# Value reload splits moved back, table loads given a later due time, and one query tile moved ahead of mixer A, in a one-core encoder layer

## The chip, the core and the metric

The kernel runs on one core of one Trainium2 chip. The metric is the device time of one execution in microseconds (us), a median over several executions. The engines are named as in the profile: PE (TensorE matmul) and PEld (its weight loads), DVE (VectorE), ACT (ScalarE), POOL (GpSimd) and SP (SyncE, which here only issues DMAs). Each engine takes its instructions in the order of the program and waits at semaphores for the others.

## The reference

One encoder layer over 512 tokens of width 1024: two token mixers side by side, merged by gates, then a SwiGLU channel mixer, with layer norm after each half.

```python
proj = h @ w_in[l]
qa, ka, va, qb, kb, vb = jnp.split(proj, SPLITS, axis=-1)
# partial rotary on qa, ka, qb, kb
o_a = windowed_gqa_sink(qa, ka, va, a_sink[l])      # 16 query heads, 4 key heads, |i-j| <= 128
o_b = dilated_mixture(qb, kb, vb)                   # 3 groups of 4 heads, strides 1, 4, 16
gates = jax.nn.sigmoid(h @ w_gate[l] + b_gate[l])
g_a, g_b = jnp.split(gates, N_BRANCH, axis=-1)
mixed = g_a * (o_a @ w_br_a[l]) + g_b * (o_b @ w_br_b[l])
h = layer_norm(DN_ALPHA * h + mixed @ w_out[l], ln1_g[l], ln1_b[l])
f = (jax.nn.silu(h @ w_ff_gate[l]) * (h @ w_ff_up[l])) @ w_ff_down[l]
h = layer_norm(DN_ALPHA * h + f, ln2_g[l], ln2_b[l])
```

## The kernel before

Everything is float32. To keep its precision on PE, each operand is split into a high part (a copy rounded to `fp32r`, L332 on ACT or L334 on DVE) and a low part (source minus high part, a subtraction on DVE), and a product is three matmuls: high by high, high by low, low by high. A dense projection of 128 output features is 8 such triples, 24 matmuls of 128x512 (`feat_k`, L453 to L455).

The kernel is written as a list of operations that a small planner (`Program.run`) puts in order when the program is built. The planner has a cost for each operation and a priority: for most, the planned PE time at which the operation was written down plus an offset (`prio`, where `EV` is -100, so "100 us early"), for some an absolute number (`abs_prio`). At each moment of its own clock it gives each engine the ready operation with the lowest number for which slots and banks are free. What comes out is one fixed order for each engine. On the chip an engine can't overtake: if the planner thought that a transfer would land earlier than it does, everything behind its reader on that engine waits.

`ORDER` is the list of steps of the first half. `q2` to `q7` and `k1` are projections for mixer A, `VA` the values of mixer A together with those of mixer B's first group, `G` and `g` a gate projection, `T` a "turn" (rotary on up to four tiles at once), and `A0` to `A3` the four key heads of mixer A with 4 query blocks each. The projections k0, q0 and q1 stand ahead of the list. The `Q`, `K`, `V` and `B` words are mixer B.

Four places matter here.

- **Tables and mask.** `ropec`, `ropes` (for the turn), `maska`, `sink`, `ident` and `bgate` are loaded through SP at L340, after the input and the first weights and close to the weights of q2 and of `VA` (L609).
- **Values and their reload.** `token_values(False)` makes four 128x512 tiles of values. Each is copied out of PSUM and stored to DRAM (`va`, L638). When all four are stored, they are read back in another order of rows: four loads of 128x256 for mixer A (L644), then eight of 64x256, two to a tile, for the first group of mixer B (L650). Each of the four tiles is then split twice by `value_split` (high part L332 or L334, low part L588): the first splits take the L644 halves and are needed by `A0`, the second splits take the L650 halves and are needed by mixer B only, some 200 us later.
- **A unit of mixer A** (`unit_a`): for each of 4 heads a pair of score matmuls (L575, L576) into a bank, a masked reduction on DVE (L724), an exponential on ACT (L728); then a reciprocal on DVE (L731) and four normalisations (L664 on ACT or L666 on DVE); then transposes on PE (L676), whose result is copied and split (L332 on ACT, L681 on DVE), and the products with the values (L741, L742).
- **The turn.** The raw rows go through SP (L482) into one tile, DVE shuffles and combines them with the tables (L493 to L499), SP moves them back (L503), and the heads are split (L525, L541).

Of the kernel before, what the change touches and what calls it, by code (L numbers as in the profile page):

```python
# [15 lines left out]
P = 128  # L16
S = 512
# [28 lines left out]
PE, ACT, DVE, POOL, SP = "PE", "ACT", "DVE", "POOL", "SP"  # L46
# [25 lines left out]


ORDER = """
q2 VA T G A0 q3 q4 G k1 T A1 q5 G q6 q7 T A2 G G A3 Q00 K00 T V Q02 K02 T Q01 K01 T B0 B1 G g Q10 K10 T g Q12 K12 T Q11 K11 T B2 B3 g8
"""


# [18 lines left out]
class Program:  # L97
# [72 lines left out]
    def run(self):  # L170
# [5 lines left out]
        dma = [0.0, 0.0]  # L176
# [22 lines left out]
        while n_left:  # L199
# [11 lines left out]
            while progress:  # L211
                progress = False
                for e in engines:
# [25 lines left out]
                    if e == SP:  # L239
                        end = now + 0.06  # L240
                        dma[0] = max(dma[0], now) + (0.45 if cost > 0.2 else 0.62)
                        dma[1] = max(dma[1], dma[0] + 0.65) + cost
                        o.done = dma[1] + 0.9
                    elif o.moves:
                        end = now + cost
                        dma[1] = max(dma[1], end) + o.moves
                        o.done = dma[1] + 2.0
                    else:
                        end = now + cost
                        o.done = end  # L250
# [28 lines left out]
def dve(n, fast=False, extra=0.0):  # L279
    return 0.069 + (0.00074 if fast else 0.00104) * n + extra  # L280
# [7 lines left out]
def hybrid_layer(ctx: ExitStack, tc: tile.TileContext, wpack, xT, xtok, sink, bgate,  # L288
# [140 lines left out]
        op([(DVE, dve(S))], lambda e, j=j, st=st: nc.vector.tensor_tensor(  # L429
            xl[j](), st.t, f32(xh[j]()), op=ALU.subtract), reads=[st, th], writes=[tl], abs_prio=ap)  # L430
    cosT, sinT, mA, mB = slot(), slot(), slot(), slot()
    for t_, src, ap in ((cosT, ropec, -119.3), (sinT, ropes, -119.2)):
        load(t_, src[0:16].unsqueeze(0).broadcast_to([8, 16, S]), abs_prio=ap)
    load(mA, maska, abs_prio=-119.3, dst=lambda: mA.t[:, :384])
    load(nsink, sink.partition_broadcast(P), 0.1, abs_prio=-119.2)
    load(ident, identd, 0.2, abs_prio=-119.1)
    load(bg, bgate, 0.1, abs_prio=-119)
    op([(DVE, 0.08)], lambda e: nc.vector.tensor_scalar(nsink.t, nsink.t, -1.0, None, op0=ALU.mult),
       reads=[nsink], writes=[nsink], abs_prio=-119)
# [23 lines left out]
        for k in range(KD):  # L463
            feat_k(ps, wu, k, XM, xtok_of)

    EV, NOW = -100.0, -300.0


    SHUF = [*range(8, 16), *range(0, 8), *range(24, 32), *range(16, 24)]
# [1 line left out]
    class Turn:  # L471
# [16 lines left out]
        def turn(self):  # L488
            n = len(self.m)
            t, w = self.t, slot()  # L490
            r = slice(0, 32 * n)
            toks = [(t, i, hh) for i in range(n) for hh in range(2)]
            op([(DVE, dve(S, extra=0.03))], lambda e: nc.vector.stream_shuffle(w.t[r], t.t[r], SHUF), reads=toks,  # L493
               writes=[w], prio=EV)
            op([(DVE, dve(S))], lambda e: nc.vector.tensor_tensor(t.t[r], t.t[r], cosT.t[r], op=ALU.mult),
               reads=[*toks, cosT], writes=[t], prio=EV)
            op([(DVE, dve(S))], lambda e: nc.vector.tensor_tensor(w.t[r], w.t[r], sinT.t[r], op=ALU.mult),
               reads=[w, sinT], writes=[w], prio=EV)
            op([(DVE, dve(S))], lambda e: nc.vector.tensor_tensor(t.t[r], t.t[r], w.t[r], op=ALU.add),  # L499
               reads=[t, w], writes=[t], prio=EV)  # L500
            for i, (raw, heads, post, args) in enumerate(self.m):
                for hh in range(2):
                    op([(SP, 0.1)], lambda e, raw=raw, a=64 * hh, d=32 * i + 16 * hh: nc.sync.dma_start(  # L503
                        raw.t[a:a + 16], t.t[d:d + 16]), reads=[t, raw], writes=[(raw, hh)], prio=EV)
                post(raw, heads, *args)
# [72 lines left out]
        return go, [(qt, "h"), (qt, "l"), (kt, "h"), (kt, "d"), (kl, "h"), (kl, "d")]  # L578


    def value_split(ps, c0, toks):

        t = slot(F32R)
        v = lambda: t.t.rearrange("p (h c) -> p h c", h=4)
        src = lambda: ps.t[:, c0:c0 + 256].rearrange("p (h c) -> p h c", h=4)
        op(cp_alts(256, True), lambda e: copy(e, v()[:, :, 0:64], src()), reads=toks,
           writes=[(t, "h"), (t, "room")], prio=EV)
        op([(DVE, dve(256))], lambda e: nc.vector.tensor_tensor(  # L588
            v()[:, :, 64:128], src(), f32(v()[:, :, 0:64]), op=ALU.subtract),
           reads=[*toks, (t, "h")], writes=[(t, "l")], prio=EV)  # L590
        return t

    def vtok(t):
# [2 lines left out]
    def token_values(dilated):  # L596
# [43 lines left out]
        if not dilated:  # L640
            raw = [slot() for _ in range(NR)]
            every = [(aside, r) for r in range(NR)]
            for m, t in enumerate(raw):
                op([(SP, 0.37)], lambda e, t=t, m=m: nc.sync.dma_start(  # L644
                    t.t[:, 0:256], aside.t[:, 32 * m:32 * m + 32, 0:256]), reads=every, writes=[(t, 0)], prio=EV)

            for m, t in enumerate(raw):
                for h in range(2):
                    c = 16 * ((2 * m - 1 + h) % 8)
                    op([(SP, 0.18)], lambda e, t=t, h=h, c=c: nc.sync.dma_start(  # L650
                        t.t[64 * h:64 * h + 64, 256:512], aside.t[:, c:c + 16, 256:512]), reads=every, writes=[(t, 1, h)],
                       prio=EV)
            for g in range(2):
                for m, t in enumerate(raw):
                    res[g].append(value_split(t, 256 * g, [(t, 1, h) for h in range(2)] if g else [(t, 0)]))
        return res


# [937 lines left out]
```

## Time and profile before

| | |
|---|---|
| median of 3 runs | 792.73 us (792.34 to 793.79) |
| profiled execution | 792.01 us, of which the span is 790.2 us |
| PE busy | 770.3 us (97%) |
| DVE, ACT busy | 651.1 us (82%), 482.6 us (61%) |
| weight loads on PE busy | 677.4 us (86%) |
| DMA queue of SP | 91.47 MB, 35.7% of 16 engines |

The span runs from the first instruction to the last; the 1.8 us that the profiled execution has over it lie around it. Times inside the span are counted from its start. In rows of the timeline the columns are start, length, engine and line, operation, out<-in with shapes, and in brackets the idle time of the engine just before, with what ended it. A matmul's length overlaps the next one: what it costs is the distance between two starts, 0.23 us for 128x512 at the full clock. A row of the windows view has the stretch, its length, and for each engine the busy time with the number of instructions, then the granted PE clock, the DMA share and GB/s. A row of the waits view has the waiting engine and line, what it waited for, and total, number and longest wait. Line numbers are those of the kernel before; in the changed kernel the same lines stand one to three further down.

### The profile page before, as it was taken

How to read it: one execution, taken by the hardware profiler on the slowest of the kernel's cores; microseconds unless marked ns; L12 is line 12 of the kernel's file. 1: busy time of each engine (PE TensorE's matmuls, PEld its weight loads, DVE VectorE, ACT ScalarE, POOL GpSimd, SP SyncE). 2: the span in 40 equal slices, each digit the busy share in tenths (PEclk: the TensorE clock that was granted, in tenths of full speed). 3: DMA queues.
4: the chain of work that ended last, by engine and by line, in shares of the span. 5: the costliest groups of instructions: out<-in, count | busy, mean ns of one | idle time of the engine just before them, and what ended most of it. 6: DMA issues, size and time to landing. Idle time of an engine off the chain costs nothing.

```text
span 790.2 us, 13367 instructions
## 1 busy us (share of the span) xinstructions
PE 770.3 (97%) x4470; PEld 677.4 (86%) x4470; DVE 651.1 (82%) x1370; ACT 482.6 (61%) x1066; POOL 124.1 (16%) x288
## 2 busy tenths in 40 slices
PE   8996999999999999999999999999999999999996
PEld 5785888888888888888888899999999999999985
DVE  5385887988899999688686999888888889788697
ACT  5455667778687787596252557655655655555631
POOL 0010000001001701600011011134112330123002
PEclk9997999999999999999999999999999999999999
DMA  7744222313132225154465188779876987689202
GB/s 243 216 151 152 84 79 93 100 46 117 38 106 92 82 82 169 55 188 158 139 206 109 50 216 251 174 171 202 221 197 149 227 203 210 168 221 201 66 1 107
DMA packets 69221, 113.36 MB, mean 143 GB/s; under 512 B 8608, under 2 KB 17440, under 8 KB 69152
## 3 DMA queue, kind: packets, MB, share of 16 engines
q1 hardware_dynamic: 57488, 91.47, 35.7%
q0 software_dynamic: 11520, 20.98, 16.3%
q8 instruction: 35, 0.57, 0.3%
q14 instruction: 34, 0.28, 0.1%
q10 hardware_dynamic: 144, 0.07, 0.0%
HBM read 104.87 MB, written 4.72 MB: 139 GB/s over the span
## 4 chain that ended last, share of the span: by engine, by line
PE 89%; DMA 5%; SPq 3%; ACT 2%; DVE 1%; issue 1%; DVEq 0%; ACTq 0%
PE ps L453 10%; PE ps L454 10%; PE ps L455 9%; PE ps L1310 9%; PE ps L1309 9%; PE ps L1308 9%; PE ps L1437 4%; PE ps L1438 4%; PE ps L1439 4%; PE ps L676 3%; PE ps L1075 3%; PE ps L1074 3%; PE ps L1073 3%; PE ps L576 1%; PE ps L575 1%; PE ps L742 1%
## 5 line engine op out<-in xcount | busy, mean ns | idle before, releaser
L332 ACT ACTIVATE sl<-sl 128x512 fp32r<-128x512 f32 (+4 forms) x452 | 243.5, 568 | 82.9 <-PE ps L454 21.3
L1192 DVE TENSOR_TENSOR sl<-sl,sl 128x512 fp32r<-128x512 f32 (+3 forms) x304 | 170.0, 604 | 10.8 <-ACT sl L332 7.5
L332 ACT ACTIVATE sl<-ps 128x256 f32<-128x256 f32 (+4 forms) x202 | 88.1, 455 | 102.0 <-PE ps L1310 66.0
L453 PE MATMUL ps<-x,sl 128*128 128x512 f32 x304 | 121.9, 401 | 1.0 <-ACT x L332 1.0
L454 PE MATMUL ps<-x,sl 128*128 128x512 f32 x304 | 119.8, 394 | 0.3 <-DVE x L429 0.2
L455 PE MATMUL ps<-x,sl 128*128 128x512 f32 x304 | 119.2, 392 | 0.0
L353 DVE TENSOR_TENSOR sl<-sl,sl 128x512 fp32r<-128x512 f32 x114 | 75.4, 686 | 8.7 <-ACT sl L332 7.9
L1262 POOL DMA_DIRECT2D sl<-wpack x44 | 40.7, 982 | 266.3 <-DVE sl L1192 109.4
L1308 PE MATMUL ps<-x,sl 128*128 128x256 f32 x264 | 74.8, 283 | 0.0
L1310 PE MATMUL ps<-x,sl 128*128 128x256 f32 x264 | 74.7, 283 | 0.0
L1309 PE MATMUL ps<-x,sl 128*128 128x256 f32 x264 | 74.7, 283 | 0.0
L1192 DVE TENSOR_TENSOR sl<-sl,ps 128x512 f32<-128x512 f32 (+1 forms) x78 | 47.4, 611 | 25.7 <-PE ps L1310 16.6
L455 PEld LDWEIGHTS ps<-x,sl 128*128 128x128 f32 x304 | 57.4, 189 | 12.7
L453 PEld LDWEIGHTS ps<-x,sl 128*128 128x128 f32 x304 | 57.7, 190 | 11.3 <-ACT x L332 1.5
L454 PEld LDWEIGHTS ps<-x,sl 128*128 128x128 f32 x304 | 57.6, 190 | 10.4 <-DVE x L429 1.2
L1309 PEld LDWEIGHTS ps<-x,sl 128*128 128x128 f32 x264 | 50.6, 192 | 0.5
L1308 PEld LDWEIGHTS ps<-x,sl 128*128 128x128 f32 x264 | 50.6, 192 | 0.5
L1310 PEld LDWEIGHTS ps<-x,sl 128*128 128x128 f32 x264 | 50.6, 192 | 0.0
L1310 PE MATMUL ps<-tw,sl 128*128 128x256 f32 x176 | 49.8, 283 | 0.0
L1309 PE MATMUL ps<-tw,sl 128*128 128x256 f32 x176 | 49.8, 283 | 0.0
L1310 PE MATMUL ps<-sl,sl 128*128 128x256 f32 x176 | 49.8, 283 | 0.0
L1308 PE MATMUL ps<-tw,sl 128*128 128x256 f32 x176 | 49.8, 283 | 0.0
(150 smaller groups left out, 1862.7 us busy)
## 6 DMA issues: line engine op xcount, KB each, us to landing
sl<-wpack SPq DMA_DIRECT2D x235, 256.0 KB
sl<-wpack POOLq DMA_DIRECT2D x44, 256.0 KB, 5.3
wf<-wpack SPq DMA_DIRECT2D x36, 256.0 KB
wf<-wpack POOLq DMA_DIRECT2D x36, 256.0 KB, 6.4
sl<-sl SPq DMA_DIRECT2D x88, 32.0 KB
sl<-wpack SPq DMA_DIRECT2D x19, 128.0 KB
sl<-xT SPq DMA_DIRECT2D x8, 256.0 KB
sl<-xtok SPq DMA_DIRECT2D x8, 256.0 KB
```

What stands on the lines that cost most here:

```text
L332: nc.scalar.activation(dst, src, AF.Copy)
L353: op([(DVE, dve(S))], lambda e: nc.vector.tensor_tensor(l.t, src.t, f32(h.t), op=ALU.subtract), reads=[src, h], writes=[l], prio=prio, abs ...
L453: mm(o, a, x0, start=(k == 0), stop=False)
L454: mm(o, a, x1, start=False, stop=False)
L455: mm(o, b, x0, start=False, stop=(k == nk - 1))
L1192: op([(DVE, dve(w))], lambda e: nc.vector.tensor_tensor(dst(), x(), y(), op=o), reads=reads, writes=writes, prio=prio)
L1262: return op([(POOL, 1.0)], lambda e: nc.gpsimd.dma_start(dst.t, wpack[u, :, j * S:(j + 1) * S], accum_op=ALU.add), reads=[dst], writes=[ds ...
L1308: mm(o, wh, bh[k](), start=(first and k == 0), stop=False, skip_group_check=True)
L1309: mm(o, wh, bl[k](), start=False, stop=False, skip_group_check=True)
L1310: mm(o, wl, bh[k](), start=False, stop=(k == 3), skip_group_check=True)
L1437: mm(ps.t, x0, w[0].t, start=(first and m == 0), stop=False, skip_group_check=True)
L1438: mm(ps.t, x0, w[1].t, start=False, stop=False, skip_group_check=True)
```

## The change

`ORDER` gets q3 ahead of `A0` instead of behind it. The second value splits get the priority `LATER` (30 us behind the place where they are written) in place of `EV`, and so, in the planner, do the loads that feed them. The planner is told that the reload takes longer: a higher cost for each transfer and 4 us more before its data are there (`READ`). The tables and the mask get `abs_prio` -95.3 to -95.1 in place of -119.3 to -119.1; the load of `bgate` keeps -119. The shuffle of the turn now names the whole tile among what it reads.

```diff
 ORDER = """
-q2 VA T G A0 q3 q4 G k1 T A1 q5 G q6 q7 T A2 G G A3 Q00 K00 T V Q02 K02 T Q01 K01 T B0 B1 G g Q10 K10 T g Q12 K12 T Q11 K11 T B2 B3 g8
+q2 VA T G q3 A0 q4 G k1 T A1 q5 G q6 q7 T A2 G G A3
+Q00 K00 T V Q02 K02 T Q01 K01 T B0 B1 G g Q10 K10 T g Q12 K12 T Q11 K11 T B2 B3 g8
 """
...
-                        o.done = dma[1] + 0.9
+                        o.done = dma[1] + 0.9 + o.moves
...
-    for t_, src, ap in ((cosT, ropec, -119.3), (sinT, ropes, -119.2)):
+    for t_, src, ap in ((cosT, ropec, -95.3), (sinT, ropes, -95.2)):
...
-    load(mA, maska, abs_prio=-119.3, dst=lambda: mA.t[:, :384])
-    load(nsink, sink.partition_broadcast(P), 0.1, abs_prio=-119.2)
-    load(ident, identd, 0.2, abs_prio=-119.1)
+    load(mA, maska, abs_prio=-95.3, dst=lambda: mA.t[:, :384])
+    load(nsink, sink.partition_broadcast(P), 0.1, abs_prio=-95.2)
+    load(ident, identd, 0.2, abs_prio=-95.1)
...
-    EV, NOW = -100.0, -300.0
+    EV, NOW, LATER, READ = -100.0, -300.0, 30.0, 4.0
...
-            op([(DVE, dve(S, extra=0.03))], lambda e: nc.vector.stream_shuffle(w.t[r], t.t[r], SHUF), reads=toks,
+            op([(DVE, dve(S, extra=0.03))], lambda e: nc.vector.stream_shuffle(w.t[r], t.t[r], SHUF), reads=[*toks, t],
...
-                op([(SP, 0.37)], lambda e, t=t, m=m: nc.sync.dma_start(
-                    t.t[:, 0:256], aside.t[:, 32 * m:32 * m + 32, 0:256]), reads=every, writes=[(t, 0)], prio=EV)
+                op([(SP, 0.6)], lambda e, t=t, m=m: nc.sync.dma_start(
+                    t.t[:, 0:256], aside.t[:, 32 * m:32 * m + 32, 0:256]), reads=every, writes=[(t, 0)], prio=EV, moves=READ)
...
-                    op([(SP, 0.18)], lambda e, t=t, h=h, c=c: nc.sync.dma_start(
+                    op([(SP, 0.75)], lambda e, t=t, h=h, c=c: nc.sync.dma_start(
                         t.t[64 * h:64 * h + 64, 256:512], aside.t[:, c:c + 16, 256:512]), reads=every, writes=[(t, 1, h)],
-                       prio=EV)
+                       prio=LATER, moves=READ)
...
-                    res[g].append(value_split(t, 256 * g, [(t, 1, h) for h in range(2)] if g else [(t, 0)]))
+                    res[g].append(value_split(t, 256 * g, [(t, 1, h) for h in range(2)] if g else [(t, 0)],
+                                              LATER if g else EV))
```

What the planner makes of it is seen in three places.

SP, where the tables are loaded. Before, from the last input tile to the first value weights:

```order
L340 DMA sl_108<-xT 128x512
L340 DMA sl_110<-ropec 128x1x512
L340 DMA sl_112<-maska 128x384
L340 DMA sl_114<-ropes 128x1x512
L340 DMA nsink<-sink 128x16
L340 DMA ident<-identd 128x128
L340 DMA bg<-bgate 128x16
L340 DMA sl_121<-maskb 128x512
L340 DMA sl_180<-wpack 128x512
L340 DMA sl_186<-wpack 128x512
L609 DMA sl_188<-wpack 128x2x128 x2
```

The same place of the change:

```order
L341 DMA sl_108<-xT 128x512
L341 DMA bg<-bgate 128x16
L341 DMA sl_111<-ropec 128x1x512
L341 DMA sl_113<-maska 128x384
L341 DMA sl_115<-ropes 128x1x512
L341 DMA nsink<-sink 128x16
L341 DMA ident<-identd 128x128
L341 DMA sl_121<-maskb 128x512
L341 DMA sl_180<-wpack 128x512
L341 DMA sl_186<-wpack 128x512
L610 DMA sl_188<-wpack 128x2x128 x2
```

The tables and the mask stay ahead of the value weights; only the 8 KB load of `bgate` changed its place. Behind this point SP's order is the same up to and with the eight loads of the reload (L650).

PE, where mixer A begins: the end of the first gate (`ps_568`) and what follows. Before:

```order
L455 MATMUL ps_568<-x_199,sl_521 128x512
L575 MATMUL ps_630<-sl_454,sl_470 128x256
L576 MATMUL ps_630<-sl_455,sl_470 128x256
L575 MATMUL ps_638<-sl_454,sl_476 128x256
L576 MATMUL ps_638<-sl_455,sl_476 128x256
L453 MATMUL ps_643<-x_128,sl_528 128x512
```

In the change (`ps_630` is now q3's bank, and the rows are the first six of its 24 matmuls):

```order
L456 MATMUL ps_568<-x_199,sl_521 128x512
L454 MATMUL ps_630<-x_128,sl_528 128x512
L455 MATMUL ps_630<-x_136,sl_528 128x512
L456 MATMUL ps_630<-x_128,sl_529 128x512
L454 MATMUL ps_630<-x_128,sl_528 128x512
L455 MATMUL ps_630<-x_136,sl_528 128x512
L456 MATMUL ps_630<-x_128,sl_529 128x512
```

All of q3 now stands ahead of the first scores. Between those first scores and the first transposes of mixer A there were 30 dense matmuls (q3 and the first 6 of q4) and 16 score matmuls; now there are the same 16 score matmuls and 27 dense ones (all of q4 and the first 3 of a gate).

ACT, up to the first normalisations (L664, in the change L666). The four tiles of the reload are `sl_616`, `sl_618`, `sl_620` and `sl_622`. Before:

```order
L332 ACTIVATE sl_700<-sl_622 128x4x64
L332 ACTIVATE sl_708<-sl_572 128x512
L332 ACTIVATE sl_717<-sl_616 128x4x64
L728 ACTIVATE sl_655,st_653<-sl_655,st_653 128x257
L728 ACTIVATE sl_693,st_715<-sl_693,st_715 128x385
L332 ACTIVATE sl_734<-sl_618 128x4x64
L664 ACTIVATE sl_641<-sl_641,st_653 128x256
L332 ACTIVATE sl_743<-sl_620 128x4x64
L664 ACTIVATE sl_647<-sl_647,st_653 128x256
L664 ACTIVATE sl_649<-sl_649,st_653 128x256
L664 ACTIVATE sl_655<-sl_655,st_653 128x256
L332 ACTIVATE sl_760<-sl_622 128x4x64
```

In the change:

```order
L333 ACTIVATE sl_707<-sl_618 128x4x64
L333 ACTIVATE sl_715<-sl_620 128x4x64
L730 ACTIVATE sl_688,st_692<-sl_688,st_692 128x257
L333 ACTIVATE sl_727<-sl_622 128x4x64
L730 ACTIVATE sl_690,st_692<-sl_690,st_692 128x257
L333 ACTIVATE sl_735<-sl_591 128x512
L730 ACTIVATE sl_694,st_692<-sl_694,st_692 128x257
L333 ACTIVATE sl_764<-sl_618 128x4x64
L666 ACTIVATE sl_682<-sl_682,st_692 128x256
L666 ACTIVATE sl_688<-sl_688,st_692 128x256
L666 ACTIVATE sl_690<-sl_690,st_692 128x256
L333 ACTIVATE sl_781<-sl_599 128x512
```

The second splits of the first two tiles stood ahead of the normalisations (`sl_717`, `sl_734`), and that of the third (`sl_743`) between the first normalisation and the other three. Now one second split on ACT, that of the second tile (`sl_764`), stands ahead of three normalisations in a row; the fourth normalisation went to DVE, behind the subtraction that ends the same split, and the second splits of the third and fourth tile come after it.

More of the change, by code (lines that the diff above doesn't have):

```diff
@@ L578, in scores, with value_split @@
         return go, [(qt, "h"), (qt, "l"), (kt, "h"), (kt, "d"), (kl, "h"), (kl, "d")]
-    def value_split(ps, c0, toks):
+    def value_split(ps, c0, toks, prio=-100.0):
         t = slot(F32R)
@@ L586, in value_split @@
         op(cp_alts(256, True), lambda e: copy(e, v()[:, :, 0:64], src()), reads=toks,
-           writes=[(t, "h"), (t, "room")], prio=EV)
+           writes=[(t, "h"), (t, "room")], prio=prio)
         op([(DVE, dve(256))], lambda e: nc.vector.tensor_tensor(
             v()[:, :, 64:128], src(), f32(v()[:, :, 0:64]), op=ALU.subtract),
-           reads=[*toks, (t, "h")], writes=[(t, "l")], prio=EV)
+           reads=[*toks, (t, "h")], writes=[(t, "l")], prio=prio)
         return t
```

## The prediction

> **What bounds the kernel now.** I read the page first, then PE's waits, then the windows, and last the timelines of PE, ACT and DVE around the one large gap.
>
> ```profile
> span 790.2 us, 13367 instructions
> PE 770.3 (97%) x4470; PEld 677.4 (86%) x4470; DVE 651.1 (82%) x1370; ACT 482.6 (61%) x1066; POOL 124.1 (16%) x288
> ```
>
> PE is busy in all but 20 us of the span. The work on PE is the same before and after, so the change can only win time in which PE stands still or runs slowly. Who makes PE wait is in the waits of PE (total, times, longest):
>
> ```profile
> PE ps L676 <- ACT sl L664: 7.8, 3, 5.8
> PE ps L626 <- ACT sl L332: 1.5, 1, 1.5
> ```
>
> The transposes of mixer A (L676) wait for the normalisations on ACT (L664). The second row is the value projection, which waits once for a weight split. The windows put a place and a clock to both:
>
> ```profile
> 30.00:37.00 7.00, 5.30 (x22) 3.85 (x21) 2.10 (x4) 2.04 (x5) 0.00 (x0) 1.00 0.59 179
> 67.60:69.80 2.20, 0.16 (x1) 0.00 (x0) 1.11 (x4) 0.93 (x4) 0.00 (x0) 1.00 0.27 93
> 69.90:80.00 10.10, 5.00 (x15) 3.70 (x16) 7.54 (x21) 8.32 (x23) 1.15 (x5) 0.50 0.50 158
> 80.30:335.00 254.70, 254.70 (x1307) 216.48 (x1306) 221.04 (x559) 188.39 (x452) 44.01 (x184) 1.00 0.28 88
> 345.00:790.20 445.20, 437.37 (x2833) 399.86 (x2831) 376.55 (x693) 243.37 (x509) 75.18 (x84) 1.00 0.65 166
> ```
>
> From 80.3 to 335 us PE never waits (254.70 busy of 254.70). Behind 345 us it idles 7.8 us in 445, most of it at the very end, and from about 350 us on the order of PE, ACT and DVE is the same in both kernels. The gap is at 67.6 to 80, and the clock is at 0.50 in most of it. PE's timeline there:
>
> ```profile
> 58.10 0.39 PE L455 MATMUL ps<-x,sl 128*128 128x512 f32 x1
> 58.33 0.28 PE L575 MATMUL ps<-sl,sl 128*128 128x256 f32 x1
> ...
> 67.37 0.39 PE L455 MATMUL ps<-x,sl 128*128 128x512 f32 x1
> 73.57 0.48 PE L676 MATMUL ps<-ident,sl 128*128 128x128 f32 x1 [5.81 <-ACT sl L664]
> 75.48 2.13 PE L676 MATMUL ps<-ident,sl 128*128 128x128 f32 x7 [1.43 <-ACT sl L664]
> 77.26 0.78 PE L453 MATMUL ps<-x,sl 128*128 128x512 f32 x1
> 77.83 0.63 PE L454 MATMUL ps<-x,sl 128*128 128x512 f32 x1
> ...
> 80.26 0.40 PE L454 MATMUL ps<-x,sl 128*128 128x512 f32 x1
> 80.49 0.39 PE L455 MATMUL ps<-x,sl 128*128 128x512 f32 x1
> ...
> 83.00 1.03 PE L676 MATMUL ps<-ident,sl 128*128 128x128 f32 x8
> ```
>
> At the full clock a dense matmul takes 0.23 us (80.26 to 80.49). Eight transposes take 0.87 (83.00 to 83.79 where the next matmul starts behind the last two, 0.11 each). Between 67.60 (67.37 and 0.23) and 80.26 PE did 8 transposes and 7 dense matmuls: 0.87 + 7 x 0.227 = 2.46 us of work in 12.66 us. **The gap costs 10.2 us.** Why ACT is late is in its own timeline:
>
> ```profile
> 65.49 0.42 ACT L332 ACTIVATE sl<-sl 128x256 fp32r<-128x256 f32 x1 [4.33 <-DMA sl<-va]
> 68.35 0.42 ACT L332 ACTIVATE sl<-sl 128x256 fp32r<-128x256 f32 x1 [1.95 <-DMA sl<-va]
> ...
> 69.77 0.94 ACT L332 ACTIVATE sl<-sl 128x256 fp32r<-128x256 f32 x2 [0.51 <-DMA sl<-va]
> 71.28 0.42 ACT L332 ACTIVATE sl<-sl 128x256 fp32r<-128x256 f32 x1 [0.57 <-DMA sl<-va]
> ...
> 72.70 0.42 ACT L332 ACTIVATE sl<-sl 128x256 fp32r<-128x256 f32 x1
> 73.02 0.49 ACT L664 ACTIVATE sl<-sl,st 128x256 f32<-128x256 f32 x1
> 74.61 0.42 ACT L332 ACTIVATE sl<-sl 128x256 fp32r<-128x256 f32 x1 [1.09 <-DMA sl<-va]
> 74.93 1.29 ACT L664 ACTIVATE sl<-sl,st 128x256 f32<-128x256 f32 x3
> 76.30 0.42 ACT L332 ACTIVATE sl<-sl 128x256 fp32r<-128x256 f32 x1
> ```
>
> The 128x256 copies are the value splits. The reloaded tiles arrive one by one, about 1.43 us apart: the first halves at 65.5, 66.9 (taken by DVE, shown below), 68.3 and 69.7, the second at 71.2, 72.7, 74.6 and at the latest 76.3. ACT and DVE take them in program order, so each exponential and normalisation behind a split waits for a landing that mixer A does not need.
>
> **The change part by part.** *Tables and mask behind the value weights.* By the order of SP this does not happen: they stay ahead, and only the 8 KB of `bgate` moves in front of them. So the wait at 33 us, the only one that earlier value weights could shorten, stays. The chain of waits shows what the swap can do:
>
> ```profile
> 13.17 7.48 DMA sl<-ropes
> 20.67 0.37 SPq L609
> ```
>
> A value-weight load is issued when `ropes` has landed; `ropes` now goes out one small load later, but one more value-weight load may go out ahead of that landing. Bounds: 0.4 us either way (0.45 us is one issue on SP); I take 0. The tables' own reader, the shuffle at 40 us, is covered by 20 us. The shuffle's extra read and the planner's costs add no instruction: 0.
>
> *q3 ahead of A0, second splits later.* Instruction counts stay; what counts is when PE reaches the transposes and when they may run. Before, PE needed 9.27 us from 58.33 to 67.60 for 30 dense and 16 score matmuls. By the order it now has 51 dense (24 + 27) and the same 16: 21 x 0.23 = 4.8 us more, so it arrives at 72.4. It isn't stopped on the way: the banks that the scores go to now are waited for at reductions that DVE, stepping through its rows, ends 2 us and more ahead of PE. q3's weights were split by 57 us, since q3 ran at 58.8 before without a wait.
>
> When may the transposes run? ACT still has one second split ahead of them, that of the second tile, whose data land at 72.7, the same time as before, since SP's order up to the reload is the same. Its step is 0.32 (72.70 to 73.02), and three normalisations follow at 0.40 each (1.29 for three): ready at 73.5, 73.9 and 74.3. The fourth is on DVE:
>
> ```profile
> 66.92 0.29 DVE L334 CAST sl<-sl 128x256 fp32r<-128x256 f32 x1 [5.29 <-DMA sl<-va]
> ...
> 73.15 0.43 DVE L588 TENSOR_TENSOR sl<-sl,sl 128x256 fp32r<-128x256 f32 x1 [0.24 <-ACT sl L332]
> 73.49 0.61 DVE L724 CUSTOM_DVE_ANT_0 sl<-ps,sl,nsink 128x384 f32<-128x384 f32 x1
> 80.66 0.74 DVE L666 TENSOR_SCALAR sl<-sl,st 128x384 f32<-128x384 f32 x2
> ```
>
> DVE has two reductions of 0.54 each to do from 72.5 on (ready when the last exponential on ACT is done), then the subtraction (0.34) and the normalisation (0.33 for 384 wide, some 0.25 for 256): 74.3. So the last of the first four transposes starts at about 74.4 instead of 72.7: **1.7 us remain.** Of the same kind, smaller: behind the normalisations ACT has a weight split (0.52) and two exponentials (0.6 each) ahead of the copies of the transposed tile (76.5), DVE ends the low part at 77.6, and PE, which by then has 13 more matmuls done, is there at 77.0; with the second product **0.5 us**. The transposes of the next block wait some **0.3 us** for their last normalisation. Together 2.5 us. Bounds for this remainder: 1.1 us (the first transpose alone, 73.5 against 72.4) and 7 us (all four behind the last landing at 76.3, and the clock lost).
>
> No single remaining wait is as long as the one that lowered the clock. By the rows that one had stood 2.2 us (67.6 to 69.8) when the clock fell to 0.50; the value projection's wait of 1.5 us left it at 1.00. So the half-speed stretch goes too.
>
> The sum against the profiled execution: 792.01 - 10.2 + 2.5 = 784.3. The median of the runs lies 0.72 above that execution, so **785.0**.
>
> [...]
>
> **What is late next, and the rivals.** PE reaches everything behind 80 us 7.7 us earlier, and DVE with 221.04 us of work in 254.70 has 13% of slack there, 10.5% in a stretch that is 7.7 us shorter. The tightest place I find is the turn of q3, q4 and k1 ahead of `A1`:
>
> ```profile
> 103.56 0.69 DVE L334 COPY sl<-ps 128x512 f32<-128x512 f32 x1 [0.15 <-PE ps L455]
> ...
> 113.32 0.69 DVE L525 TENSOR_TENSOR sl<-sl,sl 64x512 fp32r<-64x512 f32 x1
> ```
>
> From the end of k1 (103.5) to q3's first head (114.0) it takes 10.5 us. By the order PE has 33 dense matmuls, 20 transposes, 8 score and 10 value matmuls in between: 7.5 + 2.2 + 0.9 + 2.3 = 12.9 us. It is covered with 2.4 us to spare.
>
> - **Part of the wait comes back behind A0** (a late copy of k1, DVE behind its plan, or a longer wait at the first transposes, since five weight loads instead of three now follow the reload at once). For it: the planner that missed the reload by several us made this order too. Against it: PE did not wait once in the 255 us that were planned in the same manner. Price: a wait of 2 us more and 2 us of half clock: 785.0 + 4 = 789.0 (786 to 790.5).
> - **DVE becomes the bound between 80 and 335 us** and everything is given back. It would need the 33.7 us that DVE idles there to be unavoidable. Result: within 1.5 us of 792.7.
> - **Slower: the turn ahead of A1 holds PE.** PE can't pass the first scores of q3's head. The copy of k1 stands on DVE behind a dozen rows of `A0`; if it slips by x, PE waits x - 2.4 us, and with the half clock 2 us more. It is slower than before from x = 2.4 + 7.7 + 1.6 - 2 = 9.7 us; at x = 11 the time is 792.7 - 7.7 + 8.6 + 2 = 795.6.
> - **All of the gap goes**, because the second tile's landing is earlier than its reader showed: 792.7 - 10.2 = 782.5.
>
> **How the numbers follow.** Forecast 785.0 (783.5 to 786): 0.62. Part comes back: 0.18. DVE takes it all: 0.08. Slower: 0.06. Nothing remains: 0.06. A measurement of this kernel tells about 0.2% (1.6 us) from no change. Faster by more: 0.62 + 0.18 + 0.06 = 0.86; within: 0.08; slower: 0.06. The range 782.5 to 790.0 holds the forecast, the last case and most of the first rival, and both bounds of the remainder (2.5 - 7 = -4.5, so 789.5) and of the swap on SP.
>
> **What would show it.** Right: PE's waits name L676 (now three lines down) with under 2.5 us in place of 7.8; no row with a clock of 0.50 between 5 and 785 us; q3 from 58.3 to 63.8, the first transposes at 73 to 74.5, the next block's at about 81.5; PE busy without a gap from there to 335 us; the wait at 33 us as before. Wrong: half clock near 75 us, or a new wait of PE above 2 us at L575 ahead of `A1`, or DVE over 95% busy with PE waiting for it.

## The result, and the profile after

| | before | changed |
|---|---|---|
| median | 792.56 us (792.34 to 793.79, 4 runs) | 783.40 us (782.55 to 785.39, 4 runs) |
| profiled execution | 792.01 us, span 790.2 | 783.75 us, span 782.0 |
| PE idle in the span | 19.9 us | 13.0 us |

The ratio is 0.9885, 95% interval 0.9863 to 0.9907. In one of the experiments below (the cost alone) the profiled execution was disturbed from beginning to end (1548.76 us); that run's time is the median of its three others, and the times in its profile are not used.

The head of the page of the changed kernel, and who makes its PE wait (total, times, longest):

```profile
span 782.0 us, 13402 instructions
PE 769.0 (98%) x4470; PEld 675.1 (86%) x4470; DVE 646.8 (83%) x1364; ACT 484.3 (62%) x1072; POOL 125.9 (16%) x288
...
PE ps L678 <- ACT sl L666: 1.4, 1, 1.4
PE ps L627 <- ACT sl L333: 1.2, 1, 1.2
...
PE ps L454 <- ACT sl L333: 0.4, 1, 0.4
PE ps L744 <- DVE sl L683: 0.2, 1, 0.2
```

The transposes (L676 before, L678 now) waited 7.8 us in three pieces; one piece of 1.4 us is left. PE's work is the same (4470 matmuls); six instructions went from DVE to ACT. The windows of the changed kernel (stretch, length, then busy time and number for PE, PEld, DVE, ACT, POOL, then the granted clock, DMA share, GB/s):

```profile
30.00:37.00 7.00, 5.53 (x24) 4.03 (x23) 2.04 (x3) 2.35 (x4) 0.00 (x0) 1.00 0.65 187
58.00:72.00 14.00, 14.00 (x68) 11.71 (x66) 7.07 (x20) 6.42 (x17) 0.56 (x3) 1.00 0.44 155
72.00:76.00 4.00, 2.49 (x14) 1.79 (x14) 3.54 (x12) 3.36 (x10) 0.53 (x1) 1.00 0.95 252
76.00:82.00 6.00, 5.76 (x28) 4.26 (x27) 4.96 (x13) 5.97 (x14) 0.74 (x4) 1.00 0.37 120
82.00:327.00 245.00, 245.00 (x1265) 208.57 (x1264) 214.73 (x551) 188.19 (x458) 45.80 (x184) 1.00 0.29 89
```

From 58 to 72 us PE never stops; it idles 1.51 us in 72 to 76 and 0.24 in 76 to 82; the clock stays at 1.00; and from 82 to 327 us it is busy for 245.00 of 245.00. (At the very end the clock falls to 0.50 in both kernels, at 776.5 us here and at 786.7 before; PE has started its last matmul by then, at 773.9 and 782.2 us.) The rows of PE, ACT and DVE at the place itself:

```profile
71.76 0.39 PE L456 MATMUL ps<-x,sl 128*128 128x512 f32 x1
73.51 1.67 PE L678 MATMUL ps<-ident,sl 128*128 128x128 f32 x8 [1.36 <-ACT sl L666]
...
81.43 1.03 PE L678 MATMUL ps<-ident,sl 128*128 128x128 f32 x8
...
72.64 0.42 ACT L333 ACTIVATE sl<-sl 128x256 fp32r<-128x256 f32 x1 [0.97 <-DMA sl<-va]
72.97 1.29 ACT L666 ACTIVATE sl<-sl,st 128x256 f32<-128x256 f32 x3
...
73.64 0.42 DVE L589 TENSOR_TENSOR sl<-sl,sl 128x256 fp32r<-128x256 f32 x1
73.98 0.34 DVE L668 TENSOR_SCALAR sl<-sl,st 128x256 f32<-128x256 f32 x1
```

ACT stands 0.97 us for one landing (the second half of the second value tile), splits it, and only then normalises. That is the one second split that the new order left in front.

To compare stages of kernels whose orders differ, I use one measure: for each matmul, the distance to the next one's start, less the usual distance for its size (0.227 us for 128x512, 0.175 for 384, 0.119 for 256, 0.109 for 128), summed where the excess is over 0.03 us. It counts waiting and half clock together. The stages are those in which something differs; 57 to 90 us holds the first unit of mixer A, 300 to 345 the end of mixer B, 345 to 400 the start of the branches. From the traces of all runs told of here but the cost alone:

| lost time of PE, us | 0-57 | 57-90 | 90-300 | 300-345 | 345-400 | behind | sum |
|---|---|---|---|---|---|---|---|
| before | 6.3 | 10.4 | 2.5 | 1.4 | 0.1 | 1.2 | 21.9 |
| changed | 5.8 | 3.1 | 2.5 | 1.0 | 0.1 | 1.3 | 13.7 |
| changed, again | 6.8 | 4.2 | 2.5 | 0.9 | 0.0 | 1.3 | 15.7 |
| tables alone | 5.2 | 11.8 | 2.5 | 1.4 | 0.1 | 1.3 | 22.2 |
| q3 alone | 6.0 | 9.2 | 2.7 | 7.1 | 9.0 | 1.5 | 35.6 |
| q3 and due time, no cost | 5.3 | 10.6 | 2.4 | 0.9 | 0.1 | 1.3 | 20.6 |
| changed without q3 | 9.3 | 1.3 | 2.6 | 0.9 | 6.5 | 2.0 | 22.6 |
| the same, branch splits earlier | 6.7 | 2.6 | 2.6 | 0.9 | 0.0 | 1.3 | 14.1 |
| READ 6 | 6.8 | 1.9 | 2.5 | 0.9 | 0.0 | 1.3 | 13.4 |
| tables behind | 4.0 | 2.6 | 2.5 | 0.9 | 0.1 | 1.3 | 11.4 |
| READ 6, tables behind | 4.9 | 1.9 | 2.5 | 0.9 | 0.0 | 1.3 | 11.5 |
| the same, again | 3.8 | 1.6 | 2.4 | 0.9 | 0.0 | 1.3 | 10.1 |
| READ 6, tables less far behind | 4.0 | 0.9 | 2.4 | 0.9 | 0.0 | 1.3 | 9.6 |

So of the 8.2 us between the two profiles, 7.3 come from the first unit of mixer A, 0.4 from the end of mixer B, and 0.5 from the first 57 us. The last is no effect of the change: the same kernel profiled again lost 6.8 there, since landings of the first loads vary from execution to execution (one weight tile that ACT splits as soon as it lands was split at 22.18 us in the first profile and at 23.22 in the second).

### The profile page after: what moved, and what is told of

It reads as the page before. It is cut to its first block, busy times and chain, and to the rows that moved or that the text cites. A ratio compares the mean times of both kernels' runs of the same rounds, so it can differ in the third digit from the quotient of the medians.

```text
span 782.0 us, 13402 instructions
## 1 busy us (share of the span) xinstructions
PE 769.0 (98%) x4470; PEld 675.1 (86%) x4470; DVE 646.8 (83%) x1364; ACT 484.3 (62%) x1072; POOL 125.9 (16%) x288
## 4 chain that ended last, share of the span: by engine, by line
PE 91%; DMA 5%; SPq 2%; DVE 1%; issue 0%; ACT 0%; DVEq 0%
PE ps L454 9%; PE ps L455 9%; PE ps L456 9%; PE ps L1312 9%; PE ps L1311 9%; PE ps L1310 9%; PE ps L1439 4%; PE ps L1440 4%; PE ps L1441 4%; PE ps L1077 3%; PE ps L1076 3%; PE ps L1075 3%; PE ps L678 3%; PE ps L628 2%; DMA sl<-va 2%; PE ps L629 2%
## 5 line engine op out<-in xcount | busy, mean ns | idle before, releaser
L333 ACT ACTIVATE sl<-ps 128x256 f32<-128x256 f32 (+4 forms) x206 | 90.5, 457 | 107.3 <-PE ps L1312 66.3
L454 PE MATMUL ps<-x,sl 128*128 128x512 f32 x304 | 121.3, 399 | 0.4 <-ACT sl L333 0.4
L455 PE MATMUL ps<-x,sl 128*128 128x512 f32 x304 | 119.3, 392 | 0.3 <-DVE x L430 0.2
L354 DVE TENSOR_TENSOR sl<-sl,sl 128x512 fp32r<-128x512 f32 x114 | 75.6, 686 | 8.0 <-ACT sl L333 7.3
L454 PEld LDWEIGHTS ps<-x,sl 128*128 128x128 f32 x304 | 57.3, 189 | 10.6 <-ACT sl L333 1.3
L455 PEld LDWEIGHTS ps<-x,sl 128*128 128x128 f32 x304 | 57.3, 188 | 10.6 <-DVE x L430 1.6
```

Of the source, the lines that this page charges most:

```text
L333: nc.scalar.activation(dst, src, AF.Copy)
L354: op([(DVE, dve(S))], lambda e: nc.vector.tensor_tensor(l.t, src.t, f32(h.t), op=ALU.subtract), reads=[src, h], writes=[l], prio=prio, abs ...
L454: mm(o, a, x0, start=(k == 0), stop=False)
L455: mm(o, a, x1, start=False, stop=False)
```

## The experiments

The runs were made in three batches, each on a chip of its own with the kernel before beside it; the ratio is to that one. The medians of the kernel before lie within 0.5 us of each other (792.42 to 792.93), so medians of different batches compare to about that much.

The theory was this. What made PE wait was the planner's belief that the reload is there earlier than it is; with a truer time for the reload it puts the second splits behind the normalisations, and that alone is the gain. The rivals were that q3's move gives the cover, that the later due time moves the splits, and that the tables carry a part.

| kernel | median, us | ratio to before, 95% |
|---|---|---|
| q3 alone | 806.74 | 1.0184 (1.0160 to 1.0209) |
| changed without q3 | 790.64 | 0.9975 (0.9963 to 0.9988) |
| tables alone | 792.50 | 0.9995 (0.9983 to 1.0007) |
| q3 and due time, no cost | 791.29 | 0.9983 (0.9971 to 0.9994) |
| READ 6 | 782.15 | 0.9865 (0.9846 to 0.9884) |
| changed without q3, branch splits earlier | 785.07 | 0.9903 (0.9884 to 0.9922) |
| tables behind | 781.68 | 0.9869 (0.9851 to 0.9887) |
| READ 6, tables behind | 781.02 | 0.9852 (0.9833 to 0.9871) |
| cost alone | 783.59 | 0.9888 (0.9871 to 0.9905) |
| READ 6, tables less far behind | 780.14 | 0.9851 (0.9834 to 0.9868) |
| changed, again | 783.50 | 0.9895 (0.9879 to 0.9911) |
| READ 6, tables behind, again | 780.73 | 0.9857 (0.9841 to 0.9872) |

### q3 alone

```diff
 (kernel before)
-q2 VA T G A0 q3 q4 G ...
+q2 VA T G q3 A0 q4 G ...
```

> The kernel before with only the move of q3 ahead of A0. By its order ACT takes the second splits of three value tiles, the last landing at about 76 us, and then three exponentials (0.6 us each) and a weight split ahead of the first normalisations, which so come at 79 to 80 us. PE, with 24 dense matmuls more in front, arrives at the transposes at about 72.2 us and stands there 7 to 8 us, at half clock from some 2.2 us on. Theory (the planner's knowledge of the reload is what takes the stall away; q3 only decides when PE arrives): the gap costs as much as before, 791 to 794 us, and PE's wait at the transposes is 6 us or longer. Rival (q3's 4.8 us of cover is the gain): 785 to 788 us.

It took 806.74 us, 14 us more than before. PE's three longest waits in it, and the window where mixer A begins:

```profile
PE ps L454 <- DVE sl L994: 5.6, 2, 4.4
PE ps L575 <- DVE st L724: 5.0, 2, 4.6
PE ps L801 <- ACT sl L332: 3.6, 1, 3.6
...
72.00:82.00 10.00, 5.81 (x19) 4.09 (x20) 8.71 (x28) 6.55 (x20) 0.95 (x3) 0.66 0.47 149
```

At the first unit of mixer A the theory held: with q3's 24 matmuls as cover the stage still lost 9.2 us (10.4 before). But PE stood at another instruction than I expected. It waited 4.64 us for a score bank (L575), because the reductions (L724) that empty the banks stood on DVE behind splits of tiles not yet landed; the wait at the transposes was 1.0. The size was missed, too: 5.7 us more at the end of mixer B and 8.9 at the branches (the waits at L454), two stages that this edit doesn't name. In both the planner had laid out the order behind the edit anew; at the branches the next run but one shows what that does, at the end of mixer B no run takes it apart (PE waits 3.57 us there for a split on ACT).

### q3 and the later due time, without the cost of the reload

```diff
 (changed kernel)
-    EV, NOW, LATER, READ = -100.0, -300.0, 30.0, 4.0
+    EV, NOW, LATER, READ = -100.0, -300.0, 30.0, 0.0
...
-                op([(SP, 0.6)], ...
+                op([(SP, 0.37)], ...
...
-                    op([(SP, 0.75)], ...
+                    op([(SP, 0.18)], ...
```

> The changed kernel with the planner's old costs of the reload (0.37 and 0.18, and READ 0): the second splits keep their later due time, q3 stays ahead of A0. By its order ACT and DVE still take second splits ahead of the reductions, exponentials and normalisations of the first block: the due time alone does not move them, since the planner believes that the data are there. Theory (it is the time that the planner gives the reload which moves the splits): normalisations at 79 to 80 us, PE waits 6 us or more, 790.5 to 794 us. Rival (the due time moves them): as the changed kernel, 782.5 to 785.5 us.

791.29 us, and 10.6 us lost in the stage: the due time does not move the splits. PE, ACT and DVE of this kernel:

```profile
73.34 0.69 PE L576 MATMUL ps<-sl,sl 128*128 128x384 f32 x1 [4.62 <-DVE st L726]
78.70 1.74 PE L678 MATMUL ps<-ident,sl 128*128 128x128 f32 x8 [1.45 <-ACT sl L666]
...
73.60 0.42 ACT L333 ACTIVATE sl<-sl 128x256 fp32r<-128x256 f32 x1 [2.61 <-DMA sl<-va]
...
78.15 1.29 ACT L666 ACTIVATE sl<-sl,st 128x256 f32<-128x256 f32 x3
...
71.53 0.29 DVE L335 CAST sl<-sl 128x256 fp32r<-128x256 f32 x1 [0.60 <-DMA sl<-va]
...
72.80 0.48 DVE L726 CUSTOM_DVE_ANT_0 sl<-ps,sl,nsink 128x256 f32<-128x256 f32 x1
```

ACT stands 2.61 us for a second half, and the first reduction (72.80) comes behind a second half on DVE (71.53). A due time of 30 us later is no help where the planner has an idle engine and believes that the data are there: it takes what is ready. The wait is again at the scores (4.62) and then at the transposes (1.45), so the expectation of 6 us at the transposes was right in the sum only.

### The changed kernel without q3's move

```diff
 (changed kernel)
-q2 VA T G q3 A0 q4 G ...
+q2 VA T G A0 q3 q4 G ...
```

> The changed kernel with q3 put back behind A0. By its order no value split stands ahead of the first block's normalisations on ACT; PE reaches the first transposes at about 64.5 us and should wait there less than 1.5 us. Behind them the copies of the transposed tiles stand behind first splits (landings at 65.5 to 69.7 us), and later ones behind second splits (74.6 and about 76 us), so some waits of 0.5 to 1.5 us each are left, 2 to 5 us in all. Theory (late splits are the gain): 783.5 to 787 us, no stretch at half clock, or a short one. Rival (the cover of q3 is needed): PE waits 5 us or more between 64 and 78 us, 788 to 792 us.

790.64 us: the time is that of the rival, the mechanism isn't. The windows around the first unit, then PE and DVE at 349 us, where the time went:

```profile
58.00:72.00 14.00, 14.00 (x72) 12.01 (x71) 11.10 (x30) 10.11 (x27) 0.30 (x2) 1.00 0.53 173
72.00:82.00 10.00, 9.77 (x49) 7.74 (x48) 9.07 (x24) 8.39 (x21) 1.01 (x6) 1.00 0.64 176
...
353.27 0.80 PE L455 MATMUL ps<-sl,sl 128*128 128x512 f32 x1 [3.43 <-DVE sl L996]
...
347.11 5.50 DVE L354 TENSOR_TENSOR sl<-sl,sl 128x512 fp32r<-128x512 f32 x9
352.53 3.09 DVE L996 TENSOR_TENSOR sl<-tw,sl 128x512 fp32r<-128x512 f32 x5
```

The stall is gone without q3 (1.3 us lost from 57 to 90, less than the 3.1 of the changed kernel). But at the start of the branches five low parts of mixer A's output (L996) stand on DVE behind nine weight splits (L354), and PE waits 3.43 us for the first; the clock is at 0.50 from 352.4 to 359.2 us. In the changed kernel two of these five stand in front of the nine:

```profile
343.02 0.68 DVE L996 TENSOR_TENSOR sl<-tw,sl 128x512 fp32r<-128x512 f32 x1
...
344.45 0.69 DVE L996 TENSOR_TENSOR sl<-tw,sl 128x512 fp32r<-128x512 f32 x1
345.06 0.76 DVE L335 CAST sl<-sl 128x512 fp32r<-128x512 f32 x2
345.73 5.58 DVE L354 TENSOR_TENSOR sl<-sl,sl 128x512 fp32r<-128x512 f32 x9
351.23 1.28 DVE L996 TENSOR_TENSOR sl<-tw,sl 128x512 fp32r<-128x512 f32 x2
```

The run with q3 alone has the same fault (six behind the nine), the kernel before has not. Its loss in the first 57 us (9.3) is an accident of its profiled execution, which at 792.94 us was the slowest of its ten: up to there SP's and ACT's orders are those of the changed kernel. So in the changed kernel q3's move is worth 7 us after all (790.64 against 783.40), but through the order of DVE some 280 us later and not as cover.

### The same with the branch splits mended

```diff
 (the kernel above)
-    sa = [split_of(..., -20) for t in oa2 for m in range(2)]
+    sa = [split_of(..., -60) for t in oa2 for m in range(2)]
```

> The changed kernel with q3 back behind A0 (as in the run of the splits without q3) and, so that the order at the start of the branches is mended, the splits of mixer A's output due at -60 in place of -20: by its order all eight low parts then stand on DVE ahead of the nine weight splits, five of which came behind them in the run without this. Theory (q3's move is not needed for the stall; the run without it lost its gain only at 349 us, 3.4 us of waiting and 2.9 of half clock): no wait near 349 us, 781.5 to 784.5 us, as fast as the changed kernel or faster. Rival (PE meets another wait there, since the results of mixer B now come later on DVE, or it is q3 that makes the difference): 786 to 791 us.

785.07 us; the loss from 345 to 400 falls from 6.5 to 0.0 us, with all eight low parts in front of these weight splits. So the loss of the run above was this order and nothing of mixer A. The median lies 0.6 us above the expected range and 1.6 above the changed kernel's, with overlapping intervals. In its profile 2.6 us are lost from 57 to 90, the longest a wait of 0.70 for a low part on DVE.

### The cost alone

```diff
 (kernel before)
-                        o.done = dma[1] + 0.9
+                        o.done = dma[1] + 0.9 + o.moves
...
+    READ = 6.0
...
-            op([(DVE, dve(S, extra=0.03))], lambda e: nc.vector.stream_shuffle(...), reads=toks,
+            op([(DVE, dve(S, extra=0.03))], lambda e: nc.vector.stream_shuffle(...), reads=[*toks, t],
...
-                op([(SP, 0.37)], ... prio=EV)
+                op([(SP, 0.6)], ... prio=EV, moves=READ)
...
-                    op([(SP, 0.18)], ... prio=EV)
+                    op([(SP, 0.75)], ... prio=EV, moves=READ)
```

> The kernel before with only the planner's time for the reload changed (costs 0.6 and 0.75, READ 6.0); second splits due as before, q3 behind A0, tables as before. By its order no value split stands ahead of the first four normalisations on ACT, PE is at the first transposes at about 64.5 us, and the order at the start of the branches is that of the kernel before. Theory (the time that the planner gives the reload is the whole gain; q3, the due time and the tables are not needed): no stall of 2 us or more between 57 and 90 us, no half clock, 781.5 to 785.5 us. Rival (the due time or q3's cover is needed as well): a wait of 3 us or more at the transposes or the value products, 786 to 791 us.

783.59 us (782.72 to 783.92), where the changed kernel took 783.50 on the same chip. So without q3's move, without the later due time and without the tables the gain is all there. By its order ACT and DVE have no value split at all, first or second, ahead of the first block's four normalisations; where its waits lie no profile shows.

The run is not quite the cost alone, though, and two things belong to this reading. READ is 6.0 here, and the shuffle's extra read stays in. That read is no work, but it moves the order: without it, or with READ 4.0, the planner still puts the value splits behind the first normalisations, yet has the five low parts behind the nine weight splits again, the fault that cost the run without q3 its gain. Neither kernel was run. The extra read by itself doesn't take the stall away: the kernel with q3 and the due time has it and lost 10.6 us there. So what is shown is that the cost takes the stall away (10.6 us lost there with all the rest of the change and the old cost, 3.1 with the new one); that the 9 us also arrive at the end of the program hangs on the order at the branches, which several parts of the change can tip.

Against the run with READ 6 below, which has q3 ahead, the later due time and the tables' numbers as well (782.15), the intervals overlap: what these add, if anything, isn't shown (1.4 us by the medians).

### The tables

Alone, as the change has them:

```diff
 (kernel before)
-    for t_, src, ap in ((cosT, ropec, -119.3), (sinT, ropes, -119.2)):
+    for t_, src, ap in ((cosT, ropec, -95.3), (sinT, ropes, -95.2)):
...
```

> The kernel before with only the later due times of tables and mask. On SP only the 8 KB load of bgate moves ahead of the tables, the order of the other engines is that of before. Theory (this part is worth nothing but a swap on SP): 792.2 us, within 0.5 us, PE's start of mixer A's first scores at 57.9 to 58.3 us, the waits at the transposes as before (7 to 8.5 us). Rival (the value weights come earlier and the tables part carries a piece of the gain): 790.5 to 791.5 us with the wait of PE at 33 us gone.

792.50 us, ratio 0.9995 (0.9983 to 1.0007): nothing. The orders of PE, ACT and DVE are those of the kernel before to the last instruction. The wait for a value weight is there as before (1.1 us here, 1.5 then):

```profile
PE ps L676 <- ACT sl L664: 8.3, 3, 6.4
...
PE ps L626 <- ACT sl L332: 1.1, 1, 1.1
```

Then the tables really placed behind value weights, by writing their loads down inside the loop over the value weights, with the load just written as what they follow (by SP's order they then stand behind five and six of the eight pairs):

```diff
 (changed kernel, in token_values)
+                if k == 1:
+                    tables([o])
...
+    def tables(after):
+        for t_, src, ap in ((cosT, ropec, -95.3), (sinT, ropes, -95.2)):
+            load(t_, src[0:16].unsqueeze(0).broadcast_to([8, 16, S]), abs_prio=ap, after=after)
...
```

> The changed kernel with the tables and the mask written down behind the first value weights, so that by SP's order they really go out behind 5 to 7 of the 8 pairs of value-weight loads. Nothing else in the order of ACT changes up to 75 us. Theory (what these words of the change say would be worth the waits for value weights): PE's waits at 22 and 33 us (0.4 and 1.2 us) go, 781.5 to 782.8 us. Rival 1 (the wait at 33 us is for the last pairs, which wait for free buffers): 783 to 784 us. Rival 2 (the turn at 40 us or a weight behind the tables comes late): 784.5 us or more.

781.68 us. The window at 33 us, in which the changed kernel has 5.53 of 7.00 us busy:

```profile
30.00:37.00 7.00, 7.00 (x32) 5.81 (x31) 1.50 (x3) 1.23 (x2) 0.00 (x0) 1.00 0.62 184
```

The wait is gone, and with it 2 to 3 us of lost time in the first 57 us (4.0 against 5.8 and 6.8). The other profiles with the tables behind lost 4.9, 3.8 and 4.0 us there, the nine profiles of other kernels 5.2 to 9.3. In the time the step is too small to be told from the changed kernel by itself: the intervals overlap (0.9851 to 0.9887 and 0.9863 to 0.9907). So tables that really go out behind the value weights take a wait away; the later numbers of the change, which don't move them there, do nothing.

### READ 6, and the two together

```diff
 (changed kernel)
-    EV, NOW, LATER, READ = -100.0, -300.0, 30.0, 4.0
+    EV, NOW, LATER, READ = -100.0, -300.0, 30.0, 6.0
```

> The changed kernel with READ 6.0 in place of 4.0. By its order no second split is left ahead of the first block's normalisations on ACT; what they wait for last is the first split of the fourth tile (landing at 69.7 us) and one exponential: ready at 70.8 to 72.3 us, when PE arrives at about 72.0. The end of mixer B and the branch products behind it (DVE's order of splits near 340 to 355 us) stand as in the changed kernel. Theory (the wait of 1.4 us that is left is the landing of the second tile's second half, put ahead by the planner): PE's wait at the first transposes under 0.5 us, 781 to 782.5 us. Rival (the rest is something else, as the reductions on DVE): 783 to 784.5 us.

782.15 us. ACT and PE at the first transposes:

```profile
72.21 1.69 ACT L666 ACTIVATE sl<-sl,st 128x256 f32<-128x256 f32 x4
...
72.88 1.84 PE L678 MATMUL ps<-ident,sl 128*128 128x128 f32 x8
```

No second split stands in front, no wait for the normalisations is left in PE's list, and the stage loses 1.9 us in place of 3.1 and 4.2. The first transposes start at 72.88, as soon as PE is there; 0.8 us are still lost among the eight, as the four normalisations follow each other only every 0.40 us. The median lies in the range of the theory, but its interval overlaps that of the changed kernel: the gain is seen in the stage alone.

READ 6 and the tables behind, the two edits together:

> The two together: READ 6.0, and the tables behind the first value weights. If both theories hold, their gains add, since one lies at 33 us and the other at 72: 779.8 to 781.5 us. If only one holds: 781.5 to 782.8 us. If neither: 783 to 784.5 us.

The same again, with the changed kernel beside it on one chip:

> The run of READ 6.0 with tables behind once more, on the same chip as the changed kernel: 780 to 782 us, 1 to 3 us under the changed kernel.

> The changed kernel itself beside these on the same chip: 783.4 us within 1 us, 1 to 3 us above the run of READ 6.0 with tables behind (781.0).

And with the tables less far behind:

```diff
 (READ 6, tables behind, in token_values)
-                if k == 1:
+                if k == 0:
                     tables([o])
```

> The run of READ 6.0 with tables behind, but the tables go out behind 4 to 5 of the 8 pairs of value-weight loads in place of 5 to 7. The wait for a gate's weight at 49 us (1.3 us in that run's profile) should be shorter, since what follows the tables is issued earlier; the wait at 33 us may come back in part. Expected 780 to 782 us: the same within 1 us.

READ 6 with the tables behind (`k == 1`) took 781.02 and again 780.73 us; the changed kernel beside the second, 783.50. All three lie where they were expected, and the two gains do seem to add, each in its own stage of the table above. With `k == 0`, so that the tables go out two loads sooner, it is 780.14 (779.53 to 781.00). The wait for a gate's weight at 50 us fell from 1.1 us (0.7 in the second profile) to 0.3, and the one at 33 us did not come back; in time it can't be told from `k == 1`. Against the kernel before measured with them the ratios are 0.9851 (0.9834 to 0.9868) for the last and 0.9895 (0.9879 to 0.9911) for the changed kernel: the intervals don't touch, so **this version beats both kernels**, the changed one by 3.4 us. The same holds for `k == 1` (0.9857, 0.9841 to 0.9872). The windows of the `k == 0` version at the two places:

```profile
30.00:37.00 7.00, 7.00 (x33) 5.79 (x32) 1.75 (x3) 1.23 (x2) 0.00 (x0) 1.00 0.61 188
58.00:72.00 14.00, 14.00 (x73) 11.97 (x72) 10.01 (x31) 9.43 (x28) 0.68 (x4) 1.00 0.47 157
72.00:82.00 10.00, 9.93 (x50) 7.86 (x49) 8.04 (x19) 6.81 (x15) 1.52 (x4) 1.00 0.65 192
```

## Why the prediction was right, and where it was not

- **The forecast, 785.0 us in a range of 782.5 to 790.0.** 783.40 lies in the range, 0.1 us under the narrow band of 783.5 to 786. The rival that all of the gap goes (782.5) is no nearer in what it says: 3.1 us of loss are left in the stage.
- **The gap costs 10.2 us.** Right: 10.4 by the measure above, and it is where the time came from.
- **Tables: by SP's order it does not happen, 0 with 0.4 either way.** Right, alone (0.9995) and in the waits. The reading of SP's order, not of the diff, decided it.
- **PE arrives at 72.4, normalisations at 73.5, 73.9, 74.3, the last on DVE at 74.3.** Right nearly to the row: PE was there at 72.0 (71.76 and 0.23), 0.4 us early, as q3 had started at 57.96 in place of 58.3; ACT's split started at 72.64 (72.70 foretold), the transposes at 73.51, DVE's normalisation ended at 74.32 (73.98 and 0.34), the next block's at 81.43 (81.5 foretold).
- **2.5 us remain.** The sum was about right: the stage went from 10.4 to 3.1, a gain of 7.3 where 7.7 was forecast. Of its terms, the first transposes lost 2.2 us by that measure (1.5 ahead of the first, the rest among the eight), where 1.7 were foretold for a PE that arrives 0.4 us later; the value products lost 0.7 (0.5 foretold), and the next block's transposes nothing (0.3 foretold).
- **The rest of the gain was not foreseen:** 0.4 us at the end of mixer B, and 0.5 in the first loads, which is no more than their scatter. Together with the 0.4 us that the stage fell short, they turn the 784.3 that the prediction has for a profiled execution into 783.75. The other 1.1 us between 785.0 and 783.40 come from the 0.72 that it added because the median before lay that far above its profiled execution; here the median lies 0.35 below. That the errors stayed this small is partly luck.
- **The first scores don't stop PE; no turn, no DVE holds it up to 335 us.** Right in this order: 245.00 of 245.00. The kernels with q3 ahead and the splits in front show what the step rested on: there the reductions came late and PE stood 4.6 us at the scores.
- **From about 350 us on the order is the same.** Nearly: PE's order is the same from 349 us of the kernel before on, ACT's only from 362 and DVE's from 367. It cost nothing here (0.1 us lost from 345 to 400 in both kernels), but the runs with q3 alone and without q3 lost 9.0 and 6.5 us in just this place. That it went well here was luck.
- **The shuffle's extra read adds no instruction: 0.** It adds none, but it does move the order (see the cost alone), and no run has it by itself.
- **q3's move as a cause.** The prediction counted q3's 4.8 us as a part of what closes the gap, together with the splits. For the kernel that was timed the sum holds, but as a cause it is wrong: q3 alone left 9.2 us in the stage and cost 14 us in all, the changed kernel without it lost only 1.3 to 2.6 there, and the kernel with the cost and without q3's move gave the whole gain (783.59 against 783.50).
- **No remaining wait is long enough to lower the clock.** This step failed in one respect. It compared lengths of waits, 1.5 against 2.2 us. In the profile above the clock stayed at 1.00; in that of the same kernel taken again (785.72 us, the slowest of its five) it did not. PE's rows and the window:

```profile
74.63 1.67 PE L678 MATMUL ps<-ident,sl 128*128 128x128 f32 x8 [1.54 <-ACT sl L666]
...
77.19 0.63 PE L454 MATMUL ps<-x,sl 128*128 128x512 f32 x1
77.61 0.63 PE L455 MATMUL ps<-x,sl 128*128 128x512 f32 x1
...
72.00:82.00 10.00, 8.32 (x33) 6.25 (x32) 8.93 (x26) 8.61 (x24) 2.05 (x5) 0.83 0.64 195
```

A wait of 1.54 us was followed by half clock from 76.4 to 79.8 us, and the stage lost 4.2 us, 1.1 us more than in the other profile, whose wait at this place was 1.36 us. The 2 us that two of the rivals add for the half clock are an estimate, and no run shows them as such: here eight dense matmuls took 3.38 us from 76.37 to 79.75 us in place of 8 x 0.227 = 1.82, so that this stretch cost 1.6 us, and the value products behind it lost nothing, where they lost 0.7 in the other profile.

## What to carry to other kernels

Where a planner lays out the order from a cost for each transfer, correct the cost of the transfer that PE is seen to wait for first: a due time moves nothing that the planner believes ready, and more work ahead of the wait doesn't help if the late data stand in front on the helping engines. Such a planner lays out everything behind an edit anew, so compare the order down to the end of the program, at the places where an engine has a long run of work that nobody waits for (here nine weight splits), before crediting the edit with the time; even an added dependency that is no work can tip it. And check in the issuing queue's order that a load given a later number has moved at all.

## What the runs showed of the hardware

In steps of 0.1 us, and without the fall behind PE's last work at the very end of each trace, the stretches at 0.50 were: 69.9 to 80.1 us in the kernel before and 71.1 to 81.4 with the tables alone (10.2 each), 72.1 to 78.9 and 311.0 to 317.8 (6.8 each) and 365.6 to 369.0 (3.4) with q3 alone, 73.4 to 76.8 and 80.2 to 83.6 with q3 and the due time (3.4 each), 38.4 to 41.8 (3.4) and 352.4 to 359.2 (6.8) without q3, and 76.4 to 79.8 in the second profile of the changed kernel (3.4). At 0.50 the dense matmuls of that last profile start 0.43 us apart (78.04 and 78.47), at 1.00 0.23 (81.64 and 81.87).

In these traces the length of a wait does not tell by itself whether the clock falls. It fell behind a wait of 1.45 us with q3 and the due time (PE went on at 78.70, the fall came at 80.2), behind one of 1.54 us in the second profile of the changed kernel (74.63, 76.4) and behind one of 1.75 us without q3 (36.72, 38.4). It stayed at 1.00 behind 1.36 us in the first profile of the changed kernel (73.51), behind 1.48 us in the kernel before (35.25) and behind the 1.7 us for a value weight with q3 alone (at 35 us). What makes the difference no run shows: none moved a wait on purpose.
